# W_up of a two-layer hybrid encoder as seven products of block sums, in groups of 512 features

## The chip, the cores and the metric

One NeuronCore of a Trainium2 chip runs the whole program. The metric is the device time of one execution in microseconds, the median of several. A profiled execution stands beside it; all rows come from that one.

## The reference

Two layers on 512 tokens of width 1024, in float32. Each layer norms x, projects it to four token mixers and their gates, merges, adds, and then applies an MLP of width 4096:

```python
x = x + merged @ w_out[l]
hm = rms_norm(x, mlp_norm_g[l])
u = jnp.square(jax.nn.relu(hm @ w_up[l]))     # (512, 1024) @ (1024, 4096)
x = x + u @ w_down[l]                         # (512, 4096) @ (4096, 1024)
```

## The kernel before

Every float32 operand is split into a part hi and a rest lo, both in the fast matmul type, and a product is three matmuls: hi hi, hi lo, lo hi. `split` (L213) is a cast on ScalarE for hi (L215) and a subtraction on VectorE for lo (L216).

The program is written in one order, and a scheduler of the tile framework deals it out to the engines' queues, with that order as priority. Memory comes in tags: `bufs` slots for all tiles of a tag. A tile takes a slot when it is first written and gives it back when its last reader is done.

The MLP of a layer runs as follows. `add_rows` (L1086) multiplies by W_out in column chunks of 256, 384 and 384, token tile by token tile, and adds onto the rows X. `norm` (L324) scales each of four token tiles into a tile of the tag r_raw (L341), transposes it on TensorE, and splits it into h (`self.hT`): 8 blocks of 128 features by 512 tokens.

Then j goes over four quarters of the 4096 features. `up` (L1104) computes u = relu(h W_up)^2 for 1024 features, features on partitions: weights in chunks of 384 columns through the tags w_raw, w_hi and w_lo (`unit`, L242), per 128 features 8 x 3 matmuls of 512 columns into a PSUM bank, then relu and square on ScalarE (L1123, L1124). The first three feature tiles of j = 0 are done in token halves of 256 columns, so that they can begin when two token tiles are normed.

`add_product` (L1208) multiplies u of the quarter before by its part of W_down by Strassen's scheme in Winograd's form: seven products of half-size blocks, 24 matmuls of 512 columns each (L1230), from sums of blocks. The sums of u are made on VectorE (`left_sums`, tag left), those of W_down by GpSimd transfers that add HBM data onto a loaded block (`right_sums`, L1192), blocks in the tag r_raw (6 slots), their splits in r_hi and r_lo (2 slots). `run` advances it by one product after each feature tile of `up`. The last quarter goes through `add_rows` in chunks of 256, 384 and 384 columns, without block sums.

Six slots of r_raw serve norm's four tiles and W_down's blocks. PSUM has the tags mm (3 banks) and s (4).

Of the kernel before, what the change touches and what calls it, by code (L numbers as in the profile page):

```python
# [10 lines left out]
F32 = mybir.dt.float32  # L11
F32R = mybir.dt.float32r
I32 = mybir.dt.int32
AF = mybir.ActivationFunctionType
# [5 lines left out]
P = 128  # L20
# [18 lines left out]
class Weights:  # L39
# [7 lines left out]
    def add(self, layer, name, k0, kk, segs):  # L47
        n = sum(w for _, w in segs)
        off = self.size
        self.units.append((off, layer, name, k0, kk, tuple(segs), n))  # L50
        self.size += P * kk * n
        return off, n
# [22 lines left out]
EVAC = 'act'  # L75
NLO, NHI, NRAW = 4, 4, 3

NLEFT, NRIGHT, NSPLIT = 8, 6, 2
BACKLOG = 1.0
STREAM = "D0 gD1 D1 A0 A1 gD2 zD2 gD0 zD0 zD1 B0 B1 B2 gA0 zA0 gA2 C0 zA2 gA1 zA1 C1 gB1 zB1 gC1 gB2 gB0 zB0 zB2 gC0 zC1 zC0 gC2 zC2"  # L80

# [83 lines left out]
class Net:  # L165
# [155 lines left out]
        self.nc.sync.dma_start(g, gain.partition_broadcast(P))  # L321
        return g

    def norm(self, pool, X, ms, g, tag="norm_h", bufs=2):  # L324

        nc = self.nc
        hi = self.hp.tile([P, KD, S], F32R, name="h_hi", tag="h_hi")
        lo = self.hp.tile([P, KD, S], F32R, name="h_lo", tag="h_lo")
        stt = nc.vector.scalar_tensor_tensor
        for t in range(NT):  # L330
            small = lambda name: pool.tile([P, 1], F32, name=name, tag=name, bufs=4)
            v, vh, y, w = small("norm_v"), small("norm_vh"), small("norm_y"), small("norm_w")
            nc.vector.tensor_scalar(v, ms[t][0], EPS, None, op0=ALU.add)
            for part in ms[t][1:]:
                nc.vector.tensor_tensor(v, v, part, op=ALU.add)
            nc.vector.tensor_scalar(y.bitcast(I32), v.bitcast(I32), -0.5, RSQRT_MAGIC, op0=ALU.mult, op1=ALU.add)
            nc.vector.tensor_scalar_mul(vh, v, -0.5)
            for _ in range(3):
                stt(w, y, y, vh, op0=ALU.mult, op1=ALU.mult)
                stt(y, w, 1.5, y, op0=ALU.add, op1=ALU.mult)  # L340
            both = pool.tile([P, 2, S], F32, name=tag, tag=tag, bufs=bufs)  # L341
            for half in range(2):
                cs = slice(half * S, half * S + S)
                h = both[:, half, :]
                stt(h, X[t][:, cs], y, g[:, cs], op0=ALU.mult, op1=ALU.mult)
                ps = self.sps.tile([P, 4, P], F32, name="tp", tag="s")
                for j in range(4):
                    self.transpose(ps[:, j, :], h[:, j * P:(j + 1) * P])
                self.split(hi[:, half * 4:half * 4 + 4, t * P:(t + 1) * P],
                           lo[:, half * 4:half * 4 + 4, t * P:(t + 1) * P], ps)  # L350
        return hi, lo


# [732 lines left out]
    def add_rows(self, pool, X, act, layer, name, k0, ms=None, order=None, out=None, chunks=((0, 256), (256, 384), (640, 384))):  # L1086

        nc = self.nc
        for i, (c0, w) in enumerate(chunks):
            units = self.chunk(layer, name, k0, KD, [(c0, w)], order)  # L1090
            for t in range(NT):
                ps = self.mm.tile([P, S], F32, name="mm", tag="mm")
                for k, (row, hi, lo) in enumerate(units):
# [7 lines left out]
                    self.squares(pool, x, part)  # L1101
                    ms[t].append(part)

    def up(self, pool, layer, j, u):  # L1104

        nc = self.nc
        for c0, w in self.col_chunks(0, D):
            units = self.chunk(layer, "up", 0, KD, [(j * D + c0, w)])
            tiles = [self.mm.tile([P, S], F32, name="mm", tag="mm") for _ in range(w // P)] if j == 0 and c0 == 0 else None
            if tiles:  # L1110

                for ts in (slice(0, S // 2), slice(S // 2, S)):
                    for f in range(w // P):
                        self.fm_group(tiles[f][:, ts], self.hT, units, f * P, ts)
            for f in range(0, w, P):
                ft = (c0 + f) // P
                if tiles:
                    ps = tiles[f // P]
                else:
                    ps = self.mm.tile([P, S], F32, name="mm", tag="mm")  # L1120
                    self.fm_group(ps, self.hT, units, f)
                r = pool.tile([P, S], F32, name="relu", tag="relu", bufs=2)
                nc.scalar.activation(r, ps, AF.Relu)  # L1123
                nc.scalar.activation(u[:, ft, :], r, AF.Square)  # L1124
                yield

# [32 lines left out]
    def right_sums(self, pool, layer, name, k0):  # L1161
# [5 lines left out]
        for kh in range(2):  # L1167
            for nh in range(2):
                at[kh, nh] = [self.W.add(layer, name, k, kk, [(nh * n, n)])[0]
                              for k in range(k0 + kh * 4, k0 + kh * 4 + 4, kk)]  # L1170
        source = lambda off: self.ins["wflat"][off:off + P * kk * n].rearrange("(p k n) -> p k n", p=P, k=kk)

        def load(q):
            got = []
            for off in at[q]:
                raw = pool.tile([P, kk, n], F32, name="r_raw", tag="r_raw", bufs=NRIGHT)
                nc.sync.dma_start(raw, source(off))
                got.append(raw)
            return got

        def put(raws):
            got = []
            for raw in raws:
                hi = pool.tile([P, kk, n], F32R, name="r_hi", tag="r_hi", bufs=NSPLIT)
                lo = pool.tile([P, kk, n], F32R, name="r_lo", tag="r_lo", bufs=NSPLIT)
                self.split(hi, lo, raw)
                got += [(hi[:, k, :], lo[:, k, :]) for k in range(kk)]
            return got

        def add(to, q):  # L1190
            for raw, off in zip(to, at[q]):
                nc.gpsimd.dma_start(raw, source(off), accum_op=ALU.add)  # L1192

        t = load((0, 0))
        yield put(t)
# [12 lines left out]
    def add_product(self, pool, X, x, layer, name, k0):  # L1208
# [9 lines left out]
        left, right = self.left_sums(pool, x, nc.vector), self.right_sums(pool, layer, name, k0)  # L1218
        for p, ((hi, lo), w) in enumerate(zip(left, right)):

            if p in (0, 1):
                bank[p] = [self.sps.tile([P, S], F32, name="u", tag="s") for _ in range(2)]
            ps = bank[p % 2] if p < 5 else [self.mm.tile([P, S], F32, name="mm", tag="mm") for _ in range(2)]
            fresh = p in (0, 1, 5, 6)
            for k, (whi, wlo) in enumerate(w):
                first, end = fresh and k == 0, k == len(w) - 1
# [24 lines left out]
    def run(self):  # L1251
# [14 lines left out]
        for layer in range(self.depth):  # L1266
            act = self.attention(layer)
            last = layer == self.depth - 1
            with tc.tile_pool(name=f"mlp{layer}", bufs=1) as pool:
# [4 lines left out]
                ms = [[] for _ in range(NT)]  # L1274
                mine = lambda k, t: tuple(x[:, k, t * P:(t + 1) * P] for x in act)
                self.add_rows(pool, X, mine, layer, "out", 0, ms, self.merges)
                self.hT = self.norm(pool, X, ms, g, "r_raw", NRIGHT)
                if not last:
                    g = self.load_gain(pool, I["attn_norm_g"][layer + 1])
                prev = None  # L1280
                for j in range(4):
                    u = pool.tile([P, KD, S], F32, name="u", tag="u", bufs=2)
                    for i, _ in enumerate(self.up(pool, layer, j, u)):

                        if prev is not None and (j < 3 or i):
                            next(prev, None)
                    if j < 3:
                        prev = self.add_product(pool, X, u, layer, "down", j * KD)

                parts = {}  # L1290
                for kh in range(2):
                    for th in range(2):
                        parts[kh, th] = self.left_split(pool, u[:, 4 * kh:4 * kh + 4, th * (S // 2):(th + 1) * (S // 2)])
                act = lambda k, t: tuple(x[:, k % 4, t % 2 * P:t % 2 * P + P] for x in parts[k // 4, t // 2])
                ms = [[] for _ in range(NT)] if not last else None
                self.add_rows(pool, X, act, layer, "down", 3 * KD, ms, None, self.out if last else None)
                if not last:
                    xs = self.dram.tile([S, D], F32, name=f"x_save{layer}")
                    x_dram = [xs[t * P:(t + 1) * P, :] for t in range(NT)]
# [75 lines left out]
```

## Time and profile before

| | us |
|---|---|
| median of 3 runs | 1855.74 |
| lowest and highest | 1854.64, 1856.93 |
| profiled execution | 1853.6 |
| its span, first to last instruction | 1851.7 |
| MLP of layer 0, from norm's transposes to the last rows | 596 to 938 |

The span is what the rows count, from 0. A matmul's duration there includes the time to drain, so two that follow one another overlap; the distance of their starts is what one costs. PE is TensorE, PEld its weight loads, DVE VectorE, ACT ScalarE, POOL GpSimd, SP the queue of plain transfers.

### The profile page before, as it was taken

Reading aid. Unit: us, or ns where it says so; the run is one execution under the profiler, and the core shown is the slowest. Engines: PE = TensorE matmul, PEld = TensorE weight load, DVE = VectorE, ACT = ScalarE, POOL = GpSimd, SP = SyncE. Lnnn points to the kernel's source line nnn. Section 1 sums busy time; section 2 is a strip of 40 time slices with the busy share of each in tenths; the row PEclk is TensorE's granted clock in tenths of the full one; section 3 lists DMA queues with packets and bytes.
Section 4 is the critical chain, followed back from the end, with each engine's and each line's share of the span. In section 5 each row is a group of like instructions: output and inputs, shape, how many; then the busy total and the mean of one; then the engine's idle time right before and its main releaser. Section 6 shows DMA issues by size and latency. Waiting matters only on the chain.

```text
span 1851.7 us, 26873 instructions
## 1 busy us (share of the span) xinstructions
PE 1787.2 (97%) x9392; PEld 1556.9 (84%) x9392; DVE 1201.0 (65%) x2553; ACT 935.0 (50%) x1905; POOL 419.0 (23%) x1215
## 2 busy tenths in 40 slices
PE   6998999999999999999999989999999999999999
PEld 5897897887889888888999979887878898888889
DVE  6677876677665465655477878666876664565652
ACT  4565664555533454554346656645553345554541
POOL 2462254333010000010023604532422000010100
PEclk9999999999999999999999989999999999999999
DMA  4312123121324656564343211221222545565622
GB/s 164 115 53 68 60 73 93 44 69 56 90 83 154 207 124 166 129 156 105 96 153 98 76 61 52 79 72 60 73 66 73 159 151 134 149 153 165 138 82 89
DMA packets 73320, 193.91 MB, mean 105 GB/s; under 512 B 8928, under 2 KB 14048, under 8 KB 73184
## 3 DMA queue, kind: packets, MB, share of 16 engines
q1 hardware_dynamic: 66272, 167.02, 28.2%
q0 software_dynamic: 6912, 25.17, 8.0%
q8 instruction: 74, 1.21, 0.3%
q14 instruction: 62, 0.51, 0.1%
HBM read 187.97 MB, written 4.19 MB: 104 GB/s over the span
## 4 chain that ended last, share of the span: by engine, by line
PE 78%; DVE 8%; POOL 6%; issue 3%; ACT 2%; DMA 2%; SPq 1%; POOLq 0%; DVEq 0%; ACTq 0%
PE mm L285 19%; PE mm L286 19%; PE mm L287 19%; PE u L1230 9%; PE mm L1230 4%; PE tp L222 3%; PE s L604 2%; POOL rs_w_qk L235 2%; DVE w_lo L216 1%; POOL rs_y_qk L238 1%; POOL rs_w_qk L236 1%; POOL rs_w_qk L237 1%; PE y L631 1%; PE y L630 1%; DMA x<-in_x 1%
## 5 line engine op out<-in xcount | busy, mean ns | idle before, releaser
L285 PE MATMUL mm<-h_hi,w_hi 128*128 128x512 f32 (+1 forms) x1104 | 424.8, 386 | 1.8 <-DVE sig L1029 1.0
L286 PE MATMUL mm<-h_lo,w_hi 128*128 128x512 f32 (+1 forms) x1104 | 423.5, 385 | 1.7 <-DVE h_lo L216 1.4
L287 PE MATMUL mm<-h_hi,w_lo 128*128 128x512 f32 (+1 forms) x1104 | 419.6, 385 | 4.3 <-DVE w_lo L216 2.4
L216 DVE TENSOR_TENSOR w_lo<-w_raw,w_hi 128x768 fp32r<-128x768 f32 (+2 forms) x337 | 299.8, 899 | 158.5 <-ACT w_hi L215 157.1
L215 ACT CAST w_hi<-w_raw 128x768 fp32r<-128x768 f32 (+2 forms) x337 | 258.1, 774 | 232.2 <-PE mm L286 105.3
L287 PEld LDWEIGHTS mm<-h_hi,w_lo 128*128 128x128 f32 x1104 | 208.5, 189 | 44.7 <-DVE w_lo L216 3.9
L285 PEld LDWEIGHTS mm<-h_hi,w_hi 128*128 128x128 f32 x1104 | 208.6, 189 | 43.1 <-DVE sig L1029 2.9
L286 PEld LDWEIGHTS mm<-h_lo,w_hi 128*128 128x128 f32 x1104 | 209.0, 189 | 41.0 <-DVE h_lo L216 2.5
L287 PE MATMUL mm<-w_hi,h_lo 128*128 128x384 f32 (+1 forms) x576 | 190.0, 331 | 2.6 <-DVE h_lo L216 2.6
L286 PE MATMUL mm<-w_lo,h_hi 128*128 128x384 f32 (+1 forms) x576 | 189.7, 331 | 1.8 <-DVE w_lo L216 1.7
L285 PE MATMUL mm<-w_hi,h_hi 128*128 128x384 f32 (+1 forms) x576 | 189.2, 334 | 1.1 <-ACT w_hi L215 0.5
L216 DVE TENSOR_TENSOR r_lo<-r_raw,r_hi 128x1024 fp32r<-128x1024 f32 x84 | 102.7, 1223 | 130.3 <-ACT r_hi L215 130.3
L1192 POOL DMA_DIRECT2D r_raw<-in_wflat x48 | 41.6, 870 | 613.9 <-DVE r_lo L216 248.9
L235 POOL TENSOR_TENSOR rs_w_qk<-rs_y_qk 128x4 f32<-128x4 f32 (+2 forms) x216 | 61.8, 286 | 436.2 <-DVE rs_y_qk L233 300.0
L215 ACT CAST r_hi<-r_raw 128x1024 fp32r<-128x1024 f32 x84 | 88.3, 1051 | 69.2 <-PE u L1230 39.2
L286 PEld LDWEIGHTS mm<-w_lo,h_hi 128*128 128x128 f32 x576 | 110.4, 192 | 3.5 <-DVE w_lo L216 2.6
L287 PEld LDWEIGHTS mm<-w_hi,h_lo 128*128 128x128 f32 x576 | 110.1, 191 | 3.6 <-DVE h_lo L216 2.9
L285 PEld LDWEIGHTS mm<-w_hi,h_hi 128*128 128x128 f32 x576 | 110.1, 192 | 2.8 <-ACT h_hi L215 0.8
L216 DVE TENSOR_TENSOR pt_lo<-tp,pt_hi 128x256 fp32r<-128x256 f32 (+2 forms) x144 | 77.9, 552 | 39.6 <-ACT pt_hi L215 30.8
L215 ACT CAST pt_hi<-tp 128x256 fp32r<-128x256 f32 (+2 forms) x144 | 66.8, 478 | 66.4 <-PE tp L222 52.5
L1230 PE MATMUL u<-r_hi,l_lo 128*128 128x512 f32 x240 | 93.7, 390 | 0.0
L1230 PE MATMUL u<-r_lo,l_hi 128*128 128x512 f32 x240 | 93.5, 390 | 0.0
(192 smaller groups left out, 3602.5 us busy)
## 6 DMA issues: line engine op xcount, KB each, us to landing
w_raw<-in_wflat SPq DMA_DIRECT2D x248, 384.0 KB, 3.3
r_raw<-in_wflat SPq DMA_DIRECT2D x48, 512.0 KB, 3.6
r_raw<-in_wflat POOLq DMA_DIRECT2D x48, 512.0 KB, 5.8
w_raw<-in_wflat SPq DMA_DIRECT2D x88, 256.0 KB, 2.7
x<-in_x SPq DMA_DIRECT2D x8, 512.0 KB, 5.7
d_full<-in_mask_d SPq DMA_DIRECT2D x8, 448.0 KB, 4.5
x_save<-x SPq DMA_DIRECT2D x4, 512.0 KB, 4.5
x<-x_save SPq DMA_DIRECT2D x4, 512.0 KB, 5.5
```

The source lines that it names most:

```text
L215: self.nc.scalar.copy(hi, src)
L216: self.nc.vector.tensor_tensor(lo, src, hi.bitcast(F32), op=ALU.subtract)
L222: self.nc.tensor.transpose(out, in_, self.ident_r if short else self.ident)
L235: eng.tensor_tensor(w, y, y, op=ALU.mult)
L236: eng.tensor_tensor(w, w, v, op=ALU.mult)
L237: eng.tensor_scalar(w, w, -0.5, 1.5, op0=ALU.mult, op1=ALU.add)
L285: nc.tensor.matmul(ps, st[0], mv[0], start=first, stop=False)
L286: nc.tensor.matmul(ps, st[0], mv[1], start=False, stop=False)
L287: nc.tensor.matmul(ps, st[1], mv[0], start=False, stop=last)
L604: self.nc.tensor.matmul(ps, q[:, qc], k[:, kc], start=i == 0, stop=i == len(ks) - 1)
L1192: nc.gpsimd.dma_start(raw, source(off), accum_op=ALU.add)
L1230: nc.tensor.matmul(ps[q], a[:, k, toks], b, start=first and i == 0, stop=end and i == 2, skip_group_check=True)
```

## The change

W_up is multiplied by the same scheme of seven products, in groups of 512 features (`up`). A group has blocks of 512 x 256 weights; each product is 24 matmuls of 256 columns, weights stationary, h moving. The sums of h are made once a layer on VectorE (`row_sums`), from an unsplit copy of h that `norm` now also writes (`keep`); they live in the tags w_hi and w_lo, which W_up no longer needs, and one in a quarter of h itself. The sums of W_up are made by adding transfers: t goes W11, + W12, + W22, + W21, with a split after each, and a second block t3 is W12 + W22. The first 512 features of a layer stay plain (`up_first`, weights through r_raw, r_hi, r_lo). With prev, one product of W_down follows every second product. r_hi and r_lo have 4 slots instead of 2, left 6 instead of 8; W_down's last two products use the tag s. The last quarter's rows go in two chunks of 512 columns, weights through r_raw too.

```diff
-NLEFT, NRIGHT, NSPLIT = 8, 6, 2
+NLEFT, NRIGHT, NSPLIT = 6, 6, 4
...
     def norm(...)
                 self.split(hi[...], lo[...], ps)
+                if keep is not None:
+                    nc.scalar.copy(keep[:, half * 4:half * 4 + 4, t * P:(t + 1) * P], ps)
...
     def add_rows(...)
-            units = self.chunk(layer, name, k0, KD, [(c0, w)], order)
+            units = self.chunk(layer, name, k0, KD, [(c0, w)], order) if w < S else self.plain_blocks(pool, layer, name, k0, c0)
...
+    def split_block(self, pool, raw):
+        hi = pool.tile(list(raw.shape), F32R, name="r_hi", tag="r_hi", bufs=NSPLIT)
+        lo = pool.tile(list(raw.shape), F32R, name="r_lo", tag="r_lo", bufs=NSPLIT)
+        self.split(hi, lo, raw)
+        return [(hi[:, k, :], lo[:, k, :]) for k in range(raw.shape[1])]
+
+    def plain_blocks(self, pool, layer, name, k0, c0):
+        got = []
+        for k in range(0, KD, 2):
+            off, _ = self.W.add(layer, name, k0 + k, 2, [(c0, S)])
+            for i, (hi, lo) in enumerate(self.split_block(pool, self.load_block(pool, off, 2, S))):
+                got.append((k + i, hi, lo))
+        return got
+
+    def up_first(self, pool, layer, u):
+        units = self.plain_blocks(pool, layer, "up", 0, 0)
+        tiles = [self.mm.tile([P, S], F32, name="mm", tag="mm") for _ in range(3)]
+        for ts in (slice(0, S // 2), slice(S // 2, S)):
+            for f in range(3):
+                self.fm_group(tiles[f][:, ts], self.hT, units, f * P, ts)
+        for f in range(4):
+            if f == 3:
+                tiles.append(self.mm.tile([P, S], F32, name="mm", tag="mm"))
+                self.fm_group(tiles[f], self.hT, units, f * P)
+            self.squared_relu(u[:, f, :], tiles[f])
+
+    def row_sums(self, pool, raw):
+        ...
+        s1 = total(x21, x22, ALU.subtract)
+        s2 = total(s1, x11, ALU.subtract)
+        sums = [s2, total(x11, x21, ALU.subtract), total(s2, x12, ALU.add)]
+        for i, s in enumerate(sums):
+            for k, (hi, lo) in enumerate(rest):
+                self.split(hi[:, i, :], lo[:, i, :], s[:, k, :])
+        hi, lo = (x[:, 0:kh, h:] for x in self.hT)
+        self.split(hi, lo, s1)
...
-    def up(self, pool, layer, j, u):
+    def up(self, pool, layer, c0, u, ft, sums):
+        ...
+        def product(ps, left, raw, fresh):
+            right = self.split_block(pool, raw)
+            for f in range(2):
+                for k, (x, w) in enumerate(zip(left, right)):
+                    for i, (a, b) in enumerate(((1, 0), (0, 0), (0, 1))):
+                        nc.tensor.matmul(ps[:, f, :], w[a][:, f * P:(f + 1) * P], x[b], ...)
+        t = load(0, 0)
+        a = bank()
+        product(a, x11, t, True)
+        nc.scalar.copy(out[0, 0], a)
+        yield
+        add(t, 0, 1)
+        c = bank()
+        product(c, x12, load(1, 0), True)
+        stt(out[0, 0], out[0, 0], c, op=ALU.add)
+        self.squared_relu(out[0, 0], out[0, 0])
+        yield
+        b = bank()
+        product(b, s1, t, True)
+        nc.scalar.copy(out[1, 1], b)
+        add(t, 1, 1)
+        t3 = load(0, 1)
+        yield
+        add(t3, 1, 1)
+        product(a, s2, t, False)
+        nc.scalar.copy(out[0, 1], a)
+        add(t, 1, 0)
+        yield
+        product(a, s3, t3, False)
+        ...
+        product(b, s4, load(1, 1), False)
+        ...
+        product(a, x22, t, False)
+        self.squared_relu(out[1, 0], a)
...
     def add_product(...)
-            if p in (0, 1):
+            if p in (0, 1, 5, 6):
                 bank[p] = [self.sps.tile([P, S], F32, name="u", tag="s") for _ in range(2)]
...
     def run(self)
+                    if j == 0:
+                        self.up_first(pool, layer, u)
+                        sums = self.row_sums(pool, raw)
+                    for c in range(1 if j == 0 else 0, 2):
+                        for i, _ in enumerate(self.up(pool, layer, j * D + c * S, u, 4 * c, sums)):
+                            if prev is not None and (i + c) % 2:
+                                next(prev, None)
...
-                self.add_rows(pool, X, act, layer, "down", 3 * KD, ms, None, self.out if last else None)
+                self.add_rows(pool, X, act, layer, "down", 3 * KD, ms, None, self.out if last else None, ((0, S), (S, S)))
```

## Rows read from the trace of the kernel before

**Rows 1.** Engine totals of the page: busy us (share) x instructions
```profile
PE 1787.2 (97%) x9392; PEld 1556.9 (84%) x9392; DVE 1201.0 (65%) x2553; ACT 935.0 (50%) x1905; POOL 419.0 (23%) x1215
```

**Rows 2.** Busy us by window: PE, PEld, DVE, ACT, POOL, clock, DMA share, GB/s
```profile
693.00:775.00 82.00, 82.00 (x362) 67.70 (x361) 49.27 (x54) 40.02 (x49) 6.90 (x8) 1.00 0.62 154
```

**Rows 3.** Chain of waits, 650 to 700: start us, us, engine, line, count
```profile
673.43 5.45 PE u L1230 x24
...
683.42 0.46 PE u L1230 x2
```

**Rows 4.** TensorE's timeline, up's first matmuls: start us, us, line, tiles
```profile
600.07 0.28 PE L286 MATMUL mm<-h_lo,w_hi 128*128 128x256 f32 x1
...
602.94 0.28 PE L286 MATMUL mm<-h_lo,w_hi 128*128 128x256 f32 x1
```

**Rows 5.** TensorE's timeline, last rows of layer 1
```profile
1846.42 0.34 PE L285 MATMUL mm<-w_hi,l_hi 128*128 128x384 f32 x1
...
1847.47 0.34 PE L285 MATMUL mm<-w_hi,l_hi 128*128 128x384 f32 x1
```

**Rows 6.** Groups by form, 640 to 890: count | busy us, mean ns
```profile
L216 DVE TENSOR_TENSOR r_lo<-r_raw,r_hi 128x1024 fp32r<-128x1024 f32 x40 | 48.9, 1223 | 63.7 <-ACT r_hi L215 63.7
...
L1216 DVE TENSOR_TENSOR x<-x,u 128x512 f32<-128x512 f32 x36 | 23.4, 682 | 1.6 <-PE u L1230 1.5
...
L215 ACT CAST r_hi<-r_raw 128x1024 fp32r<-128x1024 f32 x40 | 42.0, 1050 | 33.5 <-PE u L1230 18.3 <-PE mm L1230 13.0 <-DMA r_raw<-in_wflat 2.1
```

**Rows 7.** Timelines of VectorE, GpSimd and ScalarE: one link of the adding transfers
```profile
744.55 1.22 DVE L216 TENSOR_TENSOR r_lo<-r_raw,r_hi 128x1024 fp32r<-128x1024 f32 x1
...
746.07 0.86 POOL L1192 DMA_DIRECT2D r_raw<-in_wflat  x1 [3.74 <-DVE r_lo L216]
...
751.65 1.05 ACT L215 CAST r_hi<-r_raw 128x1024 fp32r<-128x1024 f32 x1 [2.08 <-DMA r_raw<-in_wflat]
```

**Rows 8.** Timelines around the MLP's start, layer 0: PE, DVE, ACT, SP
```profile
596.03 1.91 PE L222 MATMUL tp<-ident,r_raw 128*128 128x128 f32 x16
...
598.28 0.61 PE L285 MATMUL mm<-h_hi,w_hi 128*128 128x256 f32 x3 [0.34 <-ACT h_hi L215]
...
600.14 0.95 DVE L216 TENSOR_TENSOR w_lo<-w_raw,w_hi 128x768 fp32r<-128x768 f32 x1
...
602.04 1.41 DVE L345 SCALAR_TENSOR_TENSOR r_raw<-x,norm_y,norm_g 128x512 f32<-128x512 f32 x2
...
604.01 1.42 DVE L345 SCALAR_TENSOR_TENSOR r_raw<-x,norm_y,norm_g 128x512 f32<-128x512 f32 x2
...
619.70 0.60 ACT L1123 ACTIVATE relu<-mm 128x512 f32<-128x512 f32 x1
...
578.43 23.01 SPq L248 DMA_DIRECT2D w_raw<-in_wflat  x8
...
601.50 2.07 SPq L1177 DMA_DIRECT2D r_raw<-in_wflat  x4
```

**Rows 9.** DMA: issues, us to landing; queues: packets, MB, share; then 610 to 630
```profile
r_raw<-in_wflat POOLq DMA_DIRECT2D x48, 512.0 KB, 5.8
...
q1 hardware_dynamic: 66272, 167.02, 28.2%
...
q0 software_dynamic: 6912, 25.17, 8.0%
...
q0 software_dynamic: 576, 2.10, 55.2%
...
q1 hardware_dynamic: 903, 2.33, 31.9%
```

**Rows 10.** Windows as in rows 2, and TensorE's timeline, around a hole
```profile
448.00:451.00 3.00, 0.53 (x6) 0.29 (x5) 0.43 (x1) 0.91 (x2) 1.76 (x9) 1.00 0.00 0
...
451.50:458.30 6.80, 6.25 (x16) 4.33 (x15) 6.54 (x12) 4.47 (x11) 1.28 (x1) 0.50 0.00 0
...
451.02 0.63 PE L222 MATMUL tp<-ident,c_rb 128*128 128x128 f32 x4 [2.49 <-DVE c_rb L988]
```

## What the change should do to the time

> **What bounds the kernel now.** I read the engine totals first: TensorE is busy for 97% of the span [rows 1]. Then I read the windows, because a change in one stage is worth what that stage is bound by. In 82 us in the middle of the MLP, TensorE has no free microsecond, VectorE is at 60%, ScalarE at 49% and the DMA engines at 62% [rows 2]. So a matmul less is time less, as long as no stall comes in its place. Busy time of a matmul is longer than its slot, so I price matmuls by the distance of starts. 24 matmuls of 512 columns follow in 5.45 us, 227 ns each [rows 3]; 24 of 256 columns take 602.94 - 600.07 = 2.87 us, 120 ns [rows 4]; six of 384 take 1.05 us, 175 ns [rows 5]. All three hold a weight load per matmul, as the new ones will.
>
> **The matmuls.** Per 512 features W_up costs now 4 feature tiles x 8 k x 3 = 96 matmuls of 512: 4 x 5.45 = 21.8 us. Seven products of 2 x 4 x 3 = 24 matmuls of 256 columns cost 7 x 2.87 = 20.1 us, so 1.7 us less, not an eighth: the shorter matmul pays 13 ns of fixed cost more often. Each layer has eight such groups, the first stays plain: 14 x 1.7 = **-23.9 us**.
>
> Beside this, the Trainium skill, "TensorE: Matmul & The Clock Gate", section "Back-to-back issue gap", gives N/2.4 + 2.5 ns for a warm matmul, 109 and 216 ns here; by it a group would save 2.4 us, and all of them 33. The rows say 120 and 227, and I go by them.
>
> **Last rows.** Per layer 96 x 120 + 192 x 175 ns = 45.1 us become 192 x 227 ns = 43.6 us: 2 x 1.5 = **-3.0 us**. Their four blocks per chunk are split while earlier products run (each lasts 1.36 us, a split slot frees as often), so I cost that at nothing; without cover it is one split, 2.3 us.
>
> **Work that moves to other engines.** Per 1024 features VectorE gets 14 splits of 1223 ns and 6 PSUM adds of 682 ns, 21.2 us; ScalarE 14 casts of 1050 ns and 6 copies of half such a tile, some 0.53 us each, 17.9 us [rows 6]. Even if nothing they replace is taken off, 49.3 + 21.2 and 40.0 + 17.9 us stay below the 78.4 us that such a stretch then lasts on TensorE (14 x 2.87 + 7 x 5.45). No engine becomes the bound by its sum; what counts is who waits.
>
> **The chain of adding transfers.** A new wait: in a group one block t is split for products 1, 3, 4 and 7, and between two of these uses lies an adding transfer into it. The trace shows the link: a split ends at 744.55 + 1.22 = 745.77, GpSimd issues the add at 746.07, and the cast that waited for its landing starts at 751.65, 5.9 us later [rows 7]. With cast and subtraction (1.05 + 1.22, 2.3 together) a link is 8.2 us, against products of 2.9. While prev is there, a product of W_down (5.45) stands between. In the second group of j = 0 there is none.
> I lay out that group, with 0 at the end of the first, plain group. That one holds all four split slots; the first frees after the first six matmuls of its last feature tile, at -5.45 + 1.36 = -4.1. Product 1's block is split till -1.8, products 1 and 2 run 0 to 5.7. The add is in at -1.8 + 5.9 = 4.1, split till 6.4: product 3 starts 0.7 late and runs to 9.3. Next add in at 12.3, split till 14.6: product 4 starts **5.3 us late**. Then 5 and 6 run, and 7 (add in at 20.5, split till 22.8) is in time. What could fill the hole? Products 5 and 6, j = 1's first ones and W_down's first stand behind product 4's split in the order of the slots. I take it that tiles of one tag get their slots in program order: the blocks of W_down (r_raw, six slots) are loaded only at 601.50, behind eight loads that started at 578.43, next to norm's third r_raw tile at 602.04, though norm needs four of the six [rows 8]. Cost 6.0 per layer, **+12.0**; between 0 (filled) and 20 (links of 10 us).
> Beside this, the Trainium skill, "DMA: Bandwidth & Descriptors", section "Anatomy of one DMA", fits 2.0 us + bytes / 436e3 per GpSimd transfer, 3.2 us for 512 KB; by it a link would be 2.6 us shorter and this item some 7 us smaller. The row has 5.9 with issue and wake-up, and adding transfers take 5.8 us to land in the median [rows 9]; the rows decide.
> For j = 1 to 3, product 4 of the first group is the tight one: its slot order lets the split for product 3 begin when product 1 ends, so product 4 can't start before 2.3 + 5.9 + 2.3 = 10.5 us after that, and TensorE has 2.87 + 5.45 + 2.87 = 11.2 us of work in between. The slack of 0.7 us is gone if the add lands a microsecond late or either split queues on ScalarE or VectorE. In the second group W_down's product lies between 3 and 4 and the slack is 6 us. Queue order: adds go from 8 to 16 per j on GpSimd's queue, where one waiting for its split holds up the next; loads share SP. I take 1.5 us per j (from 0 to 4): 6 x 1.5 = **+9.0**.
>
> **The start of the MLP.** Now up's first weights have tags of their own, and TensorE goes over to them at 598.28, right behind the transposes [rows 8]. Then they are r_raw tiles behind norm's four, so by the order of slots the scheduler places their splits behind norm's last tile. VectorE begins that at 604.01 now; without up's w_lo splits in its way (four of 0.95, one at 600.14) about 600.2. From there: two halves of the product, 1.4; transposes, 0.4; cast and the two new copies for raw, 3 x 0.6; the cast of the first block, 1.05: 604.9. The three half-token tiles take 144 x 120 ns = 17.3 us and end at 622.2; now the last of them ends just before the relu at 619.70. So 2.7 us per layer, **+5.4**; between 0 and 12 (if 604.01 stays). The copies for raw also hide nowhere else: with idle ScalarE they cost 0.6 at most.
>
> **The clock.** After a hole of 2.49 us on TensorE the granted clock was 0.50, the level of 1.2 GHz, in the stretch 451.5 to 458.3, where TensorE worked for 6.25 us and lost about half of that; before and behind it was 1.00 [rows 10]. The hole before product 4 and the one at the start (597.9 to 604.9, with a few transposes) are longer. Part of such a stretch falls on waiting: I take 1.7 us for each of four, between 0 and 3.1: **+6.8**.
> The first projection of layer 1 has its weight slots earlier and the last transfer is a third larger; under 1 us each, against each other.
>
> **Sum:** -23.9 - 3.0 + 12.0 + 9.0 + 5.4 + 6.8 = +6.3. The profiled execution took 1853.6 (span 1851.7 and 1.9 around it), so 1859.9; the median of the runs, 1855.74, lies 2.1 above it: **1862 us**, slower by a third of a percent.
>
> **Rivals.**
> A. The holes are filled (faster). If the slots don't hold later products back, products 5 and 6, j = 1's and W_down's run in the hole, and the clock stays up. For it: in the chain of this trace a product of W_down is cut, 2 of its 24 matmuls ahead of the others [rows 3], so the order is dealt out finely, and TensorE has no idle time in the middle of the MLP [rows 2]. Against: that finely dealt order never had a chain with 8.2 us between products of 2.9. Then -26.9 + 3 + 5.4 = -18.5: 1837.
> B. The DMA engines bound j = 1 to 3 (slower). From the queue totals [rows 9] an added MB takes 0.080 x 1851.7 / 25.17 = 5.9 us of all 16 engines, a loaded one 0.282 x 1851.7 / 167.02 = 3.1. Per j W_up comes to 4.2 MB loaded and 4.2 added, W_down the same: 8.4 x 9.0 = 75.6 us in 78.4. Between 610 and 630, with four adds and the loads around them, both queues held 87% of the engines [rows 9]; if that is all that can be had, a j lasts 75.6 / 0.87 = 87 us, 5.3 more than the 15 x 5.45 = 81.7 of now. It decides from 71 us of packets per j on (0.87 x 81.7, what a j lasts now); the packets in that 20 us stretch, 5.3 and 2.7 us per MB, give only 67, which speaks against it. With the holes: 6 x 5.3 - 3.4 - 3.0 + 12.0 + 5.4 + 6.8 = +49.6: 1905.
> C. The clock holds and the start is half as late (3 us in all): -26.9 + 12.0 + 9.0 + 3.0 = -2.9, so 1853, no change that can be told.
> D. The matmuls of 256 don't hold 120 ns beside casts and adds: at 130 ns a group saves nothing. The 256-column rows stand in a stretch in which both other engines work, so I give it little.
>
> **How the numbers follow.** Under 0.2% (3.7 us) a measurement can't tell from no change, so the bounds are 1852 and 1859.5. Forecast 0.47 (its own range 1852 to 1880, of which 0.06 is below 1859.5), A 0.25, B 0.10, C 0.13 (0.10 same, 0.03 faster), D 0.05. Faster 0.28, same 0.16, slower 0.56. The range 1834 to 1888 leaves out B (0.10), what of A lies below 1834 (0.07) and the far ends of the unknown waits (0.03).
>
> **What would show it.** Right: in the profile after, TensorE's share falls below 97%; the 256-column matmuls of the new line stand 120 ns apart; ahead of one product in the second group of each layer TensorE is idle for some 5 us, ended by r_lo, and PEclk falls behind it; up's first matmul comes 6 to 7 us after the last transpose of norm's second tile. GpSimd issues 104 adds instead of 48, and the DMA share of the middle windows goes from 0.62 to 0.85 or more. Wrong: no hole there (A), or holes ahead of nearly every product with r_hi released by a DMA (B).

## The result and the profile after

| | before | changed |
|---|---|---|
| median, us | 1856.34 | 1911.27 (1907.55 to 1916.28) |
| span of the profiled execution | 1851.7 | 1909.4 |

The ratio is 1.030, with a 95% interval of 1.027 to 1.032: slower by 3%, where 0.3% was forecast. The time lies above the range (1834 to 1888) and next to rival B's 1905.

The page's engine totals and DMA queues of the changed kernel, beside [rows 1, 9]:

```profile
PE 1790.3 (94%) x10208; PEld 1584.0 (83%) x10208; DVE 1290.8 (68%) x2619; ACT 1003.8 (53%) x1983; POOL 469.4 (25%) x1271
...
q1 hardware_dynamic: 59936, 167.02, 26.5%
q0 software_dynamic: 14976, 54.53, 16.3%
```

TensorE's idle part of the span grows by 55 us, from 64 to 119, and the adding transfers (q0) go from 25 to 54.5 MB. Three windows show j = 1 to 3 of layer 0 (columns as in [rows 2]). Each starts with the first matmul of a j; the last ends at the first matmul of the last rows:

```profile
661.65:749.14 87.49, 81.55 (x506) 73.14 (x505) 59.38 (x62) 49.71 (x61) 13.88 (x16) 0.98 0.84 199
749.14:835.96 86.82, 81.31 (x505) 72.69 (x504) 58.76 (x62) 46.90 (x57) 13.91 (x16) 0.98 0.83 193
835.96:921.96 86.00, 82.35 (x505) 73.85 (x504) 61.80 (x65) 50.80 (x63) 12.14 (x14) 0.96 0.85 209
```

A j lasts 86.7 us on the mean of both layers, where it lasted 81.6 and 78.4 was forecast. TensorE is idle for 4 to 6 us of each, and part of the rest runs at the lower clock level.

**The second group of j = 0** went as laid out. VectorE, GpSimd, ScalarE and TensorE, as in [rows 7]:

```profile
639.02 1.23 DVE L216 TENSOR_TENSOR r_lo<-r_raw,r_hi 128x1024 fp32r<-128x1024 f32 x1 [0.85 <-ACT r_hi L215]
...
640.53 0.85 POOL L1116 DMA_DIRECT2D r_raw<-in_wflat  x1 [6.92 <-DVE r_lo L216]
...
646.24 2.94 ACT L215 CAST r_hi<-r_raw 128x1024 fp32r<-128x1024 f32 x3 [2.21 <-DMA r_raw<-in_wflat]
...
643.01 0.28 PE L1195 MATMUL mm<-h_hi,r_hi 128*128 128x256 f32 x1
643.13 0.28 PE L1195 MATMUL mm<-h_lo,r_hi 128*128 128x256 f32 x1
648.59 0.58 PE L1195 MATMUL mm<-w_hi,r_lo 128*128 128x256 f32 x1 [5.18 <-DVE r_lo L216]
```

The split of t ends at 640.25, and the cast behind the add starts at 646.24, 6.0 later (forecast 5.9). Product 4 finds TensorE idle for 5.18 us (forecast 5.3), nothing else fills the hole, and the matmuls of 256 columns stand 120 ns apart.

**The start of the MLP**, TensorE and ScalarE:

```profile
597.94 1.91 PE L222 MATMUL tp<-ident,r_raw 128*128 128x128 f32 x16
601.73 1.32 PE L222 MATMUL tp<-ident,r_raw 128*128 128x128 f32 x8 [1.89 <-ACT h_raw L352]
606.39 1.94 PE L222 MATMUL tp<-ident,r_raw 128*128 128x128 f32 x8 [3.33 <-DVE r_raw L345]
609.10 0.58 PE L285 MATMUL mm<-h_hi,r_hi 128*128 128x256 f32 x1 [0.77 <-ACT r_hi L215]
...
608.00 1.05 ACT L215 CAST r_hi<-r_raw 128x1024 fp32r<-128x1024 f32 x1
```

and the window at the lower clock:

```profile
604.10:614.30 10.20, 7.14 (x32) 6.77 (x33) 8.51 (x14) 7.22 (x11) 0.00 (x0) 0.50 0.63 207
```

W_up's first matmul comes 11.2 us behind the first of these transposes; it was 2.3 [rows 8]. The first cast of its weights (608.00) stands behind the first of the two casts of norm's last tile, as forecast. On top, the third tile's transposes wait for the new copies for raw (`h_raw`), which hold the PSUM bank, and the fourth for norm on VectorE. The granted clock is 0.50 for 10.2 us, the 1.2 GHz level.

**Ahead of W_down's products** TensorE now waits in every j. GpSimd, ScalarE and TensorE at one such place, and TensorE at another:

```profile
707.96 0.86 POOL L1116 DMA_DIRECT2D r_raw<-in_wflat  x1 [7.97 <-DMA r_raw<-in_wflat]
709.29 1.76 POOL L1116 DMA_DIRECT2D r_raw<-in_wflat  x2 [0.47 <-issue]
711.40 0.86 POOL L1116 DMA_DIRECT2D r_raw<-in_wflat  x1 [0.35 <-issue]
...
716.88 1.04 ACT L215 CAST r_hi<-r_raw 128x1024 fp32r<-128x1024 f32 x1 [4.66 <-DMA r_raw<-in_wflat]
...
717.98 0.73 PE L1323 MATMUL u<-r_hi,l_hi 128*128 128x512 f32 x2 [0.86 <-ACT r_hi L215]
...
678.79 0.91 PE L1323 MATMUL u<-r_hi,l_hi 128*128 128x512 f32 x2 [2.87 <-ACT r_hi L215]
```

Four adds are issued within 3.4 us and land 6.4, 7.5, 9.2 and 10.4 us after issue, one every 2.5 us. In j = 1 to 3 of both layers every hole over 0.15 us stands ahead of a product of W_down, none ahead of one of W_up. These holes, up to 4 us long, come to 5.1 us per j. The stretches at 0.50 behind them last 4.0 us per j, of which by estimate half is lost (matmuls of 256 columns stand 0.21 us apart at 0.50, 0.12 at 1.00). Together that is some 7 of the 8 us that a j is too long.

One whole chain in layer 1, on VectorE, SyncE's queue, GpSimd, ScalarE and TensorE: a split ends at 1643.29, which gives a slot of r_raw back; the load that waited for the slot starts; the add onto it is issued only when the load has landed, and lands 8.4 us later; then come the cast and the product:

```profile
1642.07 1.22 DVE L216 TENSOR_TENSOR r_lo<-r_raw,r_hi 128x1024 fp32r<-128x1024 f32 x1
...
1643.31 2.60 SPq L1111 DMA_DIRECT2D r_raw<-in_wflat  x2
...
1648.71 1.76 POOL L1116 DMA_DIRECT2D r_raw<-in_wflat  x2 [0.79 <-DMA r_raw<-in_wflat]
...
1657.17 1.04 ACT L215 CAST r_hi<-r_raw 128x1024 fp32r<-128x1024 f32 x1 [6.29 <-DMA r_raw<-in_wflat]
...
1658.27 0.79 PE L1323 MATMUL u<-r_hi,l_hi 128*128 128x512 f32 x2 [2.49 <-ACT r_hi L215]
```

Why the adds land so late, and what the slots have to do with it, is the question of the experiments.

### The profile page after: what moved, and what is told of

The parts are those of the page before. It is cut to its first block, busy times and chain, and to the rows that moved or that the text cites. A ratio compares the mean times of both kernels' runs of the same rounds, so it can differ in the third digit from the quotient of the medians.

```text
span 1909.4 us, 28729 instructions
## 1 busy us (share of the span) xinstructions
PE 1790.3 (94%) x10208; PEld 1584.0 (83%) x10208; DVE 1290.8 (68%) x2619; ACT 1003.8 (53%) x1983; POOL 469.4 (25%) x1271
## 4 chain that ended last, share of the span: by engine, by line
PE 58%; DMA 14%; DVE 10%; POOL 7%; issue 6%; ACT 4%; SPq 0%; POOLq 0%; ACTq 0%; DVEq 0%
PE mm L285 14%; PE mm L286 14%; PE mm L287 14%; DMA r_raw<-in_wflat 13%; PE u L1323 4%; PE mm L1195 4%; PE tp L222 4%; DVE r_lo L216 2%; ACT r_hi L215 2%; PE s L606 2%; POOL rs_w_qk L235 2%; POOL rs_w_qk L237 1%; POOL rs_w_qk L236 1%; POOL rs_y_qk L238 1%; PE y L632 1%
## 5 line engine op out<-in xcount | busy, mean ns | idle before, releaser
L216 DVE TENSOR_TENSOR r_lo<-r_raw,r_hi 128x1024 fp32r<-128x1024 f32 x206 | 248.6, 1221 | 179.6 <-ACT r_hi L215 178.8
L215 ACT CAST r_hi<-r_raw 128x1024 fp32r<-128x1024 f32 x206 | 212.0, 1048 | 204.0 <-DMA r_raw<-in_wflat 147.6
L285 PE MATMUL mm<-h_hi,w_hi 128*128 128x512 f32 x544 | 217.6, 401 | 1.1 <-DVE sig L1031 1.0
L287 PE MATMUL mm<-h_hi,w_lo 128*128 128x512 f32 x544 | 213.9, 399 | 4.6 <-DVE w_lo L216 2.5
L286 PE MATMUL mm<-h_lo,w_hi 128*128 128x512 f32 x544 | 215.4, 397 | 0.0
L1323 PE MATMUL u<-r_hi,l_hi 128*128 128x512 f32 x336 | 128.2, 401 | 25.1 <-ACT r_hi L215 25.1
L1195 PE MATMUL mm<-h_lo,r_hi 128*128 128x256 f32 x448 | 127.2, 284 | 0.0
L1195 PE MATMUL mm<-h_hi,r_hi 128*128 128x256 f32 x448 | 127.0, 284 | 0.0
L1195 PE MATMUL mm<-h_hi,r_lo 128*128 128x256 f32 x448 | 126.2, 282 | 0.7 <-DVE r_lo L216 0.6
L286 PEld LDWEIGHTS mm<-h_lo,w_hi 128*128 128x128 f32 x544 | 103.3, 190 | 20.4
```

The source lines that it names most:

```text
L215: self.nc.scalar.copy(hi, src)
L216: self.nc.vector.tensor_tensor(lo, src, hi.bitcast(F32), op=ALU.subtract)
L285: nc.tensor.matmul(ps, st[0], mv[0], start=first, stop=False)
L286: nc.tensor.matmul(ps, st[0], mv[1], start=False, stop=False)
L287: nc.tensor.matmul(ps, st[1], mv[0], start=False, stop=last)
L1195: nc.tensor.matmul(ps[:, f, :], w[a][:, f * P:(f + 1) * P], x[b], start=fresh and f + k + i == 0, stop=k == kh - 1 and i == 2, skip_group_ ...
```

## The experiments

The length of a j is the mean of six (both layers), from start to start as above; "group 2" is the second group of j = 0, from its first matmul to the first of j = 1; "add" is the median time from issue to landing of the 512 KB adding transfers between 665 and 880 us; "DMA" the busy share of the 16 engines in j = 1 to 3, mean of both layers. Each adding transfer counted is one of W_down, of W_up, or of both, as the kernel has them.

| kernel | us | a j | group 2 | add | DMA |
|---|---|---|---|---|---|
| before | 1856 | 81.6 | | 5.7 | 0.54 |
| changed | 1911.3 | 86.7 | 28.0 | 6.4 | 0.83 |
| noadd_up | 1847.7 | 78.7 | 19.9 | 5.6 | 0.66 |
| quarter_up | 1857.4 | 80.6 | 20.9 | 5.6 | 0.72 |
| quarter_down | 1879.2 | 81.0 | 28.1 | 6.4 | 0.72 |
| dump_up | 1886.9 | 84.9 | 20.2 | 6.0 | 0.88 |
| dump_sp | 1869.4 | 82.5 | 19.9 | 8.1 | 0.86 |
| start | 1899.3 | 86.4 | 28.9 | 6.5 | 0.84 |
| pool8_l5 | 1897.1 | 85.7 | 25.4 | 5.6 | 0.59 |
| pool_start | 1885.1 | 85.9 | 25.4 | 5.6 | 0.59 |
| vec_half | 1872.6 | 85.3 | 20.7 | 5.6 | 0.73 |
| vec_all | 1851.3 | 80.9 | 20.7 | 5.5 | 0.62 |
| vec_all_49 | 1837.6 | 78.7 | 20.7 | 5.9 | 0.64 |
| after_49 | 1888.7 | 82.1 | 28.2 | 7.5 | 0.85 |
| vec_half_49 | 1844.3 | 80.6 | 20.7 | 5.6 | 0.76 |

### Are the adding transfers of W_up the cause?

```diff
-        add = lambda raw, r, c: self.add_block(raw, at[r, c], kh, n)
+        add = lambda raw, r, c: None
```

> All adding transfers of W_up are left out (t is split again as it is, so W_up's sums are not formed); splits, casts, products and W_down's adds stay. Changed kernel: 1911, with holes of 36.5 us on TensorE in j = 1 to 3, 11.1 us before product 4 of j = 0's second group, and some 9 us of low clock behind these. Theory T (the adding transfers, by their time on the DMA engines or by the chain): all three go, 1911 - 57 = 1854, the holes at the start of the MLP stay. Rival S (the extra splits on ScalarE and VectorE are late): the holes in j = 1 to 3 stay, above 1890.

1847.7, ratio 0.995 (0.993 to 0.998). All holes but those at the start are gone, with all splits still there: a j lasts 78.7, near the 78.4 that the matmuls alone were forecast to take. Rival S falls. Windows as above:

```profile
665.00:745.00 80.00, 80.00 (x517) 73.09 (x516) 62.03 (x65) 49.72 (x59) 7.79 (x9) 1.00 0.65 158
745.00:825.00 80.00, 80.00 (x517) 73.09 (x517) 60.62 (x64) 47.73 (x57) 6.92 (x8) 1.00 0.66 160
```

Next, a quarter of the bytes in W_up's adds, and, the other way round, in W_down's:

```diff
+        def add(raw, r, c):
+            self.nc.gpsimd.dma_start(raw[:, 0:1, :], self.source(at[r, c], kh, n)[:, 0:1, :], accum_op=ALU.add)
```

> Each add of W_up brings only one of its four rows of blocks, 128 of 512 KB (sums of W_up only formed in that part); number of adds, waits and queue order unchanged. Theory B: per j the packets fall from 75.6 us by 3/4 of 4.2 MB x 5.9 to 57, the holes in j = 1 to 3 go, and the one before product 4 shrinks as far as the add lands earlier: 1857 to 1865. If an add's landing is mostly a fixed price per transfer (5 us and more of its 5.4 for 512 KB), the links of the chain stay at 8 us and so does the hole before product 4: above 1885.

> Each add of W_down brings a quarter of its block (128 of 512 KB; sums of W_down only formed in that part); W_up's adds are whole again. Theory B: the packets of a j fall by 3.15 MB x 5.9 = 18.6 us as in quarter_up, the holes in j = 1 to 3 go though W_up's chain is as it was; the hole of 5.3 us before product 4 of j = 0, where no W_down runs, stays, with its clock: 1911 - 36 - 5 = 1870. Theory C (chain of W_up): holes of about the same length stay in j = 1 to 3, now ahead of W_up's products 3 and 4: above 1890.

1857.4 and 1879.2. In both most of the loss in j = 1 to 3 goes. In quarter_down W_up's chain is whole, the holes of group 2 stay as they were, and yet a j falls from 86.7 to 81.0: the latency of W_up's chain is not what makes the holes of j = 1 to 3. In quarter_up W_down's adds are whole, and land in 5.6 again. Issues between 665 and 880 us, with KB and median us to landing, of quarter_up, then of quarter_down:

```profile
r_raw<-in_wflat POOLq DMA_DIRECT2D x22, 512.0 KB, 5.6
r_raw<-in_wflat POOLq DMA_DIRECT2D x21, 128.0 KB, 3.9
```

```profile
r_raw<-in_wflat POOLq DMA_DIRECT2D x21, 512.0 KB, 6.4
r_raw<-in_wflat POOLq DMA_DIRECT2D x23, 128.0 KB, 4.8
```

### Load on the DMA engines without the chain

A first try, copies from HBM to HBM in the place of the adds, told nothing.

> As noadd_up, but in the place of each add of W_up GpSimd issues a copy of the same 512 KB from HBM to HBM that nobody waits for (sums of W_up not formed). The load on the DMA engines and on GpSimd's queue stays near that of the changed kernel, the chain split, add, split is gone. Theory B (the time of the DMA engines bounds j = 1 to 3): the holes ahead of W_down's products stay, a j lasts 85 us or more, DMA share 0.8: 1911 - 11 - 4 = 1896 or more. Theory C (the latency of the chain of W_up's adds): the holes go as in noadd_up, within 6 us of it, 1854 to 1860.

1946.7: nothing held these copies back, so GpSimd issued them in the first stages, which became 100 us longer, and j = 1 to 3 ran without them. The page's rate of transfer in 40 slices shows it in the first three:

```profile
GB/s 333 266 169 108 58 74 50 75 68 58 70 71 83 133 152 120 183 142 152 174 109 109 93 89 51 68 72 44 98 62 53 90 141 119 141 162 169 147 184 53
```

So the copies were tied to the cast of the split block, once on GpSimd, once on SyncE:

```diff
+        def add(raw, r, c):
+            for _ in range(2):
+                spare = self.dram.tile([P, kh, n], F32R, name="spare", tag="spare", bufs=8)
+                nc.gpsimd.dma_start(spare, dumps[-1])
```

> In the place of each add of W_up, GpSimd copies the hi part of the block just split to HBM, twice (2 x 512 KB; sums of W_up not formed). It waits for the cast as the add waits for the split, so it comes at the same times, and loads the DMA engines about as an add does (a plain 512 KB takes 1.3 to 1.6 us of the 16 engines, an add 2.6 to 3.1); but no split waits for it, W_up has no chain. Theory B (W_down's adds land late because the DMA engines are full): W_down's adds land in 7 us or more in the median, a j lasts 84 us or more, the hole before product 4 of j = 0 is gone: 1911 - 11 - 4 = 1896 (1885 to 1915). Theory C (the chain of W_up's adds makes the holes, and its lateness passes on): no holes in j = 1 to 3, as noadd_up, 1848 to 1856.

> As dump_up, but the two copies to HBM are issued by SyncE, on the queue of the plain loads, so that GpSimd's queue holds W_down's adds alone (sums of W_up not formed). Theory B1 (the 16 DMA engines are shared, whichever queue the packets come from): a good part of W_down's adds of j = 1 to 3 lands late again (7 us or more; in noadd_up 1 of 22, in dump_up 8 of 22), holes ahead of W_down's products, 1870 to 1900. Theory B2 (transfers wait for those ahead of them on GpSimd's own queue): W_down's adds land in 5.3 to 6 us as in noadd_up, and holes, if any, are released by plain loads. SyncE waits for each cast before its copies, which may hold loads behind them back: that would show as loads issued late, not as adds landing late.

1886.9, inside the range of theory B, and 1869.4, just under that of B1. W_up has no chain, and the holes ahead of W_down's products are back in both: theory C falls. With the copies on SyncE's queue W_down's adds, alone on theirs, land in 8.1 us, so B2 can't be the whole cause: the engines are shared. (Trainium skill, "DMA: Bandwidth & Descriptors", section "Queues, rings and completion order": each engine takes turns between the queues that have work for it. The trace agrees: 5.6 us without the copies, 8.1 with them on the other queue.) Queue shares and issues of dump_sp between 665 and 880 us:

```profile
q1 hardware_dynamic: 11926, 43.43, 57.5%
q0 software_dynamic: 3168, 11.54, 29.4%
...
spare<-r_hi SPq DMA_DIRECT2D x40, 512.0 KB, 6.9
r_raw<-in_wflat POOLq DMA_DIRECT2D x22, 512.0 KB, 8.1
```

The order within a queue counts too. In dump_up, where the median is 6.0, one add is issued ahead of four copies and lands in 5.5 us; the next, behind them, takes 10.9, and a product waits for it. GpSimd, ScalarE and TensorE:

```profile
696.94 0.90 POOL L1116 DMA_DIRECT2D r_raw<-in_wflat  x1 [10.70 <-DMA r_raw<-in_wflat]
697.51 2.47 POOL L1191 DMA_DIRECT2D spare<-r_hi  x4
699.62 1.28 POOL L1116 DMA_DIRECT2D r_raw<-in_wflat  x1
...
710.58 1.99 ACT L215 CAST r_hi<-r_raw 128x1024 fp32r<-128x1024 f32 x2 [2.21 <-DMA r_raw<-in_wflat]
...
711.68 0.73 PE L1332 MATMUL u<-r_hi,l_hi 128*128 128x512 f32 x2 [2.75 <-ACT r_hi L215]
```

The longest hole of each j in dump_up stands behind such an add of 10.7 to 11.3 us; the holes of dump_sp are shorter, behind adds of 8.3 to 10.6. So the median landing doesn't tell how long a j is. Nor does the share of the engines: vec_half (below) needs 85.3 at 0.73. What sets it is how late W_down's blocks come.

### The start

```diff
+                units = self.plain_blocks(pool, layer, "up", 0, 0)
                 self.hT = self.norm(pool, X, ms, g, "r_raw", NRIGHT, raw)
...
-        units = self.plain_blocks(pool, layer, "up", 0, 0)
```

> The first weights of W_up (plain blocks) are put in the program ahead of norm instead of behind it; nothing is left out. Changed kernel: TensorE's first matmul of W_up 11.2 us behind the start of the transposes of the second pair of tiles (2.3 before the change), then 10.2 us at the low clock. Theory: the casts and splits of these weights stand behind norm's fourth tile only by program order: first matmul within 4 us, the clock stays up, 1911 - 2 x (7 + 5) = 1887. Rival: norm's own work with the extra copies of h (8 of 0.6 us on ScalarE, which also hold the banks of the transposes) sets the start: at most 2 x 2.5 us less, 1906.

1899.3, half of what was expected. TensorE, as above:

```profile
597.35 1.91 PE L222 MATMUL tp<-ident,r_raw 128*128 128x128 f32 x16
600.10 0.61 PE L285 MATMUL mm<-h_hi,r_hi 128*128 128x256 f32 x3 [0.84 <-ACT h_hi L215]
```

The first matmul now comes after 2.75 us and the clock stays up, so program order was the cause. But the 5 us of clock were counted wrongly: from W_up's first matmul to group 2 it still takes 25.4 us, because the last two tiles' transposes and the waits for them now lie in there. From the transposes to group 2 it is 8.3 us less in layer 0 and 7.7 in layer 1. Of these 16 us 12 arrive: the stage between the two MLPs takes 575.7 us instead of 571.9, for a reason that stays open.

### The sums without adding transfers

With the sums on GpSimd, from blocks that are loaded anyway, alone and with the start:

```diff
+        gadd = lambda raw, other: self.nc.gpsimd.tensor_tensor(raw, raw, other, op=ALU.add)
...
-NLEFT, NRIGHT, NSPLIT = 6, 6, 4
+NLEFT, NRIGHT, NSPLIT = 5, 8, 4
```

> W_up's sums by GpSimd's arithmetic in SBUF, from the four blocks that are loaded anyway, in place of adding transfers (8 slots of r_raw, 5 of left; nothing left out). A 128x512 addition on GpSimd takes 1.53 us in the trace of before, so 3.1 for a block, and a link of the chain 2.3 + 3.1 + 0.3 = 5.7 us instead of 8.2; per j 8 of them, 25 us of GpSimd. Theory B: the adds' 4.2 MB x 5.9 = 25 us per j are gone from the DMA engines, no holes in j = 1 to 3 and under 1 us before product 4: as noadd_up, 1848 to 1854. Rival: VectorE slows down beside GpSimd's arithmetic (its 128x1024 subtraction over 1.4 us), or the slots of r_raw hold the loads back: 1865 or more.

> As pool8_l5, and the first weights of W_up ahead of norm in the program (as in start; nothing left out). In start the first matmul of W_up came 8.4 us sooner and the 10.2 us of low clock there (5 us lost) were gone, per layer, but the whole gained only 12 us, since the DMA engines' time in j = 1 to 3 gave part of it back. Theory B: with the DMA engines free all of it counts: pool8_l5 less 2 x 13 us, 1822 to 1828. If the gain there was half for another reason, 1836 to 1842.

1897.1 and 1885.1: the rival won. Groups of VectorE and GpSimd in pool8_l5, 660 to 900, count | busy us, mean ns:

```profile
L216 DVE TENSOR_TENSOR r_lo<-r_raw,r_hi 128x1024 fp32r<-128x1024 f32 x78 | 107.8, 1401 | 46.3 <-ACT r_hi L215 45.9
...
L1186 POOL TENSOR_TENSOR r_raw<-r_raw 128x1024 f32<-128x1024 f32 x22 | 61.8, 2808 | 83.2 <-DVE r_lo L216 82.7
```

A subtraction takes 1.40 us on the mean instead of the 1.22 of [rows 6], and VectorE is busy 70 us in the 88 from 661 to 749. (Trainium skill, "SBUF — State Buffer", section "Who interferes with whom": a VectorE instruction with both inputs in SBUF contends with a GpSimd instruction that reads SBUF. The trace agrees: 1.40 us beside GpSimd's sums, 1.22 without.) The DMA engines are at 0.59, where they were at 0.54 before the change, and a j still takes 85.7. Both halves of the rival meet in its longest holes: at 717.70 TensorE waits for a block of W_down whose load started at 703.12, when a subtraction of 3.4 us had given a slot back.

In pool_start the start of each layer is 8.1 us shorter than in pool8_l5, and again 12 us of 16 arrive, with the stage between the MLPs 573.7 instead of 569.6. So it isn't the DMA engines' load in j = 1 to 3 that took the other 4 in the run start, as the expectation had it.

With the sums on VectorE instead, half of them or all in j = 1 to 3, and all in j = 0:

> VectorE makes W_up's sums from the loaded blocks: all four in j = 0, two of four (t + W12, t3 = W12 + W22) in j = 1 to 3, the other two by adding transfers; first weights of W_up ahead of norm (8 slots of r_raw, 5 of left; nothing left out). Per j VectorE's busy time, 60 us in the changed kernel, becomes 65 of 78; the packets 75.6 - 2.1 MB x 5.9 = 63 us. Theory B: few holes in j = 1 to 3 (quarter_up, with 57 us, had 7 us in two layers), no hole before product 4: quarter_up's 1857 less 2 x 8 for the start, 1835 to 1848, faster than before the change. Rival (the chain of W_down is late through VectorE, as in pool8_l5, where it was busy 70 of 87 us): 1860 or more.

> As vec_half with all four sums on VectorE in every group; no adding transfer of W_up is left. VectorE 60 + 8 x 1.22 = 70 of 78 us per j, the packets 51 us. Theory B: holes only where VectorE's queue makes a split late: noadd_up's 1848 less 2 x 8 for the start, 1828 to 1842. Rival (VectorE's queue): 70 us of it were too much in pool8_l5 (holes of some 16 us per layer in j = 1 to 3), 1860 or more.

1872.6, in the rival's range, and 1851.3, in neither; vec_all's ratio is 0.998 (0.996 to 0.999). Group 2 has no hole of 5 us any more, but in vec_half a j is as long as with GpSimd. VectorE does more in vec_all, whose j is shorter, so its load is not what holds vec_half up. What is left stands mostly at one place per j, in both. Queue of SyncE, GpSimd, ScalarE and TensorE in vec_all:

```profile
689.80 0.33 SPq L1112 DMA_DIRECT2D r_raw<-in_wflat  x1
...
695.85 0.86 POOL L1117 DMA_DIRECT2D r_raw<-in_wflat  x1 [6.40 <-DMA r_raw<-in_wflat]
...
703.00 2.00 ACT L216 CAST r_hi<-r_raw 128x1024 fp32r<-128x1024 f32 x2 [6.90 <-DMA r_raw<-in_wflat]
...
704.10 0.50 PE L1339 MATMUL u<-r_hi,l_hi 128*128 128x512 f32 x1 [1.78 <-ACT r_hi L216]
```

W_down's t3 is loaded, added onto, and split, one behind the other, and its load starts only when a slot of r_raw is free.

```diff
-NLEFT, NRIGHT, NSPLIT = 5, 8, 4
+NLEFT, NRIGHT, NSPLIT = 4, 9, 4
```

> As vec_all with 9 slots of r_raw and 4 of left instead of 8 and 5 (nothing left out). In vec_all TensorE still waits some 6 us in layer 0 and 4 in layer 1 in j = 1 to 3, at one place per j: the load of W_down's t3 starts only when a split gives a slot of r_raw back (689.80), its add follows at 695.85 and lands at 702.93, cast and subtraction end at 705.3, 15.5 us in all. Theory (slots): with one more the load starts a step earlier, these holes go, 1851 - 10 = 1841 (1838 to 1846). Rival (VectorE, busy 70 of 80 us per j, or the fewer slots of left, set these steps): 1850 or more.

1837.6, ratio 0.990 (0.988 to 0.992): **1% faster than the kernel before**. VectorE is busy for 70 of 80 us, and TensorE has no hole:

```profile
665.00:745.00 80.00, 80.00 (x512) 72.83 (x510) 70.32 (x73) 48.89 (x59) 8.00 (x10) 1.00 0.68 171
745.00:825.00 80.00, 80.00 (x511) 72.89 (x510) 69.30 (x70) 47.86 (x58) 6.92 (x8) 1.00 0.64 160
```

### How the loss divides

> The changed kernel with 9 slots of r_raw and 4 of left instead of 6 and 6, nothing else. It loses 26 us of TensorE's time per layer in j = 1 to 3, with 16 adding transfers per j. Theory N (the number of adding transfers: W_down's adds land late among W_up's, slots or not): about as now, 1895 to 1915, half of W_down's and W_up's adds landing in over 6.4 us. Theory R (the slots of r_raw: loads start too late for the adds that follow them, as in vec_all): most of the loss goes, 1865 to 1880.

> vec_half (two of W_up's four sums by adding transfers in j = 1 to 3) with 9 slots of r_raw and 4 of left. vec_half loses 22 us per layer in j = 1 to 3, vec_all 8, and vec_all with these slots 2. Theory N: the two adds left per group keep most of the loss: 1860 or more. Theory R: with the slots it goes as in vec_all, within some 6 us of its 1838: 1838 to 1848.

1888.7, between the two theories' ranges, and 1844.3, in that of theory R. With slots alone, a j of the changed kernel falls from 86.7 to 82.1 at the same DMA share, though the adds land later still (7.5): over half of the 8 us goes. With half the adds and nine slots 1.9 are left, with none 0. Six slots cost nothing as long as W_up adds nothing (noadd_up). So neither is the cause alone: an add that lands late holds its slot longer, the next load starts later, and the add behind it too. The run after_49 still loses 3.4 us per j; whether to the engines' rate, to the order in GpSimd's queue or to slots that are still too few stays open.

## Why the prediction was wrong

The sum was +6.3; the spans differ by 57.6. Term by term, from the starts of matmuls, both layers (a j and group 2 are set against noadd_up, which has no holes there):

| term | forecast | measured |
|---|---|---|
| W_up's matmuls | -23.9 | -22.7 |
| last rows | -3.0 | -3.6 |
| start, with its clock | +8.8 | +16.0 |
| group 2, with its clock | +15.4 | +16.1 |
| j = 1 to 3, with its clock | +9.0 | +47.9 |
| the rest | 0 | +3.9 |

**Matmuls, last rows:** right. A j without holes is 78.7 (forecast 78.4, though 14 x 2.87 + 7 x 5.45 gives 78.3) and group 2 19.9 us; the last rows take 43.5 us instead of 45.3. In noadd_up and vec_all_49 a j has this length.

**Engines by their sums:** right. 62 us of VectorE and 50 of ScalarE in 80 give no hole (noadd_up).

**Group 2:** right in place, cause and size, clock included. The order of the slots does hold later products back, and rival A falls with that.

**The step that failed: "I take 1.5 us per j"**, which measured 8.0. The prediction followed W_up's chain through j = 1 to 3 and expected the hole ahead of W_up's product 4. W_down's chain, which adds onto two blocks at a time through the same queue, the same engines and the same six slots, was taken over as it was, with the 5.8 us of [rows 9] to a landing. There was the least slack: every hole stands there. Four of its and W_up's adds in a row land up to 10.4 us after issue, and the six slots carry each delay on. Nine slots alone take away 4.6 of the 8.0 us (after_49); leaving W_up's adds out takes away all of them (noadd_up). "Adds go from 8 to 16 per j" stood in the text as a matter of the queue's order; what it does to the landing of the other chain wasn't worked out, though [rows 9] show that four adds and the loads around them already held 87% of the engines.

**Rival B** came within 7 us of the time, with a j of 87 (86.7 measured), and was given 0.10. That its size fits is in part luck. The engines are shared, and that delays the adds, but no limit of 87% sets the changed kernel's j. B's sum hangs on the bytes alone, and after_49 moves the same bytes in 82.1 us per j. The changed kernel itself stays below the limit (0.83), dump_up goes above it (0.88), and vec_half, at 0.73, is nearly as slow. Whether the engines' rate has a part in what after_49 still loses, at 0.85, isn't shown.

**Start:** the place was right (weights behind norm's last tile), the size 8.0 per layer instead of 4.4. VectorE was to begin norm's last tile at 600.2, 4.2 us behind the first transposes; it began 7.6 us behind them (605.49), though W_up's splits were out of its way. What the sum left out are the third tile's transposes, which wait for the copies for raw: that these "cost 0.6 at most" was wrong, since they hold the banks.

**Clock:** holes of 1.8 to 5.2 us were followed by 3.4 to 6.8 us at 0.50, though not each of them: one of 2.7 us in layer 1 was not. With the 10.2 us at the start there are five stretches in each layer's MLP, 27.3 us, in the place of the two that were counted.

Where the rest, 3.9 us, comes from stays open. Ahead of the first MLP it is 1.9; the stage between the two MLPs took 570.3 us before, 571.9 in the changed kernel, and 569.6 (pool8_l5) to 578.5 (vec_all_49) in the other runs, whose edits lie in the MLP. So part of what vec_all_49 saves in the MLP is lost there.

## What to carry to other kernels

When a change adds work to a shared resource, follow every chain that already runs through it, not only the new one: the one with the least slack pays. A sum that needs a load, an adding transfer and a split one behind the other has a latency that here rose with the adds under way; more buffers let it start sooner, and making the sum on an engine that still had room took it away. Bytes over capacity say that waiting is near, not how long it will be.

## What the runs showed of the hardware

An adding transfer of 128 KB lands in 2.8 us at the least (quarter_up), one of 512 KB in 5.1 to 5.3: by estimate about 2.0 fixed and 0.8 per 128 KB. (Trainium skill, "DMA: Bandwidth & Descriptors", section "Anatomy of one DMA": 2.0 us + bytes / 436e3, by estimate 2.3 and 3.2 for these sizes. The fixed part agrees, the slope of an adding transfer is over twice as steep.) An f32 addition of 128x1024 on GpSimd takes 2.81 us, and VectorE's subtractions beside such additions are 15% longer on the mean (pool8_l5); the same addition on VectorE takes 1.2 (vec_all).
